# First two channel groups of an input projection computed side by side, with earlier requests for weights and rows

## The chip, the cores and the metric

The kernel runs on one core of a Trainium2 chip. The metric is the device time of one execution in microseconds (us). Five engines take part, each with its own instruction queue that runs in order: PE (TensorE: matmuls and transposes), ACT (ScalarE), DVE (VectorE), POOL (GpSimd) and SP (SyncE, which here only requests DMA transfers). An instruction that has to wait holds up everything behind it in its queue.

## The reference

One layer of a bidirectional encoder on 2048 rows of 1024 channels. Two head groups share one input projection: four mLSTM heads and a Hyena operator (long two-sided convolutions by FFT). An output projection and an MLP follow.

```python
hn = rms_norm(x, norm_mix_pre)
proj = (hn @ w_in).astype(f32)                       # 1024 -> 3600 columns
cv = short_conv3(proj[..., :N_CONV], conv_w, conv_b) # the first 2560 columns, 3 taps along the rows
q, k = silu(cv[..., 0:512]), silu(cv[..., 512:1024]) * D ** -0.5
v, o_gate, gates = proj[..., 2560:3072], sigmoid(proj[..., 3072:3584]), proj[..., 3584:3600] + b_gates
h_m = (mlstm_chunkwise(q, k, v, ...) + flip(mlstm_chunkwise(flip(q), ...))) * o_gate
z = cv[..., 1024:1536]                               # Hyena value, then two gates
z = cv[..., 1536:2048] * two_sided_fft_conv(z, filt[:, 0, 0], filt[:, 1, 0], fb[0])
z = cv[..., 2048:2560] * two_sided_fft_conv(z, filt[:, 0, 1], filt[:, 1, 1], fb[1])
mix = concat([group_rms(h_m), group_rms(z)]) @ w_out
x = x + rms_norm(mix, norm_mix_post)
x = x + rms_norm(square(relu(rms_norm(x) @ w_mlp_in)) @ w_mlp_out)
```

## The kernel before

**Normalisation (`normalise`, L489).** The 2048 rows are 16 tiles of 128 rows. A tile is fetched on SP (`xt`, four buffers), squared and summed on ACT (L516), scaled on DVE (L520), and turned by eight PE transposes (L484) in two halves of four; each half is copied out of PSUM by ACT as a rounded high part (L486) and by DVE as the low part (L487). Four tiles make one row block: `hn[b]`, b = 0 to 3, high and low. The PSUM ring of the transposes holds three halves, so a fourth half waits until ACT and DVE have emptied the first. The short convolution's weights (`cw`, four loads with single elements of 4 bytes) are requested in this stage too.

**Input projection (`convolved`, L559).** 2560 of the columns are 20 channel groups of 128. One block is a group times a row block: 8 steps of k, each three matmuls (L159 low weights, L160 low rows, L161 high times high), so 24 matmuls of 512 columns. Blocks run group by group, and within a group over the four row blocks. ACT starts the convolution of a finished block (L590), DVE adds the two side taps (L596), four PE transposes turn it (L617, the first 12 groups), ACT copies it out (L626), POOL stores it. `in_weights` (L530) fetches a group's weights in two halves (`wf`, two buffers), POOL scales them by the norm's weights (L543), ACT and DVE split them into high and low (L166, L169).

**Fillers and leads.** `project` is a Python generator: the 80 blocks, then `values_project` (the other 1040 columns, 64 blocks of 24 matmuls of 260 columns, in four sets, the first of which needs 4 weight parts to begin), each step yielding a cost. It is the filler beside three leads. During `normalise` every even step p takes three steps of it (one block, L527). Beside `filters` (the Hyena filter spectra; its small matmuls stand at L393) and `long_conv` (the two long convolutions) the function `drive` (L217) advances the filler until its summed cost has caught up with the lead's:

```python
self.drive(work, (1.55 * n for n in self.filters(c2, consts)))
with tc.manual_schedule():
    self.drive(work, self.long_conv(hyp, hy, early))
    for _ in work:
        pass
```

What filler is left when `long_conv` is through is emitted behind it. At the end of `long_conv` its buffers are given back, and `head_loads` requests the k, v and q of mLSTM head 0, 1 MB each, into that space; `turned` then transposes k (L912). The mLSTM stage follows (state updates L932, scores L964, outputs L981 and L982), fed by broadcast loads `mb` and `qs` of 0.5 MB each, whose space is that of the projection's tiles. Before `manual_schedule` a scheduler sets the order of the instructions on each engine; inside it the program's order stands.

Of the kernel before, what the change touches and what calls it, by code (L numbers as in the profile page):

```python
# [8 lines left out]
F32 = mybir.dt.float32  # L9
F32R = mybir.dt.float32r  # L10
AF = mybir.ActivationFunctionType
ALU = mybir.AluOpType
# [135 lines left out]
class Builder:  # L148
# [340 lines left out]
    def normalise(self, c, conv):  # L489

        tc, io = self.tc, self.io
        act, dve = self.act, self.dve
        wk = c.enter_context(tc.tile_pool(name="nwk", bufs=2))
        ps = c.enter_context(tc.tile_pool(name="nps", bufs=3, space=PSUM, side="right"))
        xs = {}

        def fetch(t):
            xs[t] = wk.tile([128, D], F32, tag="xt", name="xt", bufs=4)
            self.load(xs[t], io["x"][0, 128 * t:128 * t + 128, :])

        fetch(0)
        fetch(1)
        self.load(self.nw, io["norm_mix_pre"].rearrange("(k p) -> p k", p=128))
        for p in range(9):
            if p == 2:
                for n in range(3):
                    self.load(self.cw[:, :, n], io["conv_w"][n].rearrange("(t p) -> p t", p=128))
                self.load(self.cw[:, :, 3], io["conv_b"].rearrange("(t p) -> p t", p=128))
            if p < 8:
                if p < 7:  # L510
                    fetch(2 * p + 2)
                    fetch(2 * p + 3)
                ss = wk.tile([128, 2], F32, tag="ss", name="ss")
                for i in range(2):
                    junk = wk.tile([128, D], F32, tag="junk", name="junk", bufs=1)
                    act.activation(junk, xs[2 * p + i], AF.Square, accum_out=ss[:, i:i + 1])  # L516
                r = self.rstd(wk, ss, D, 2, "pre")
                for i in range(2):
                    xt = xs[2 * p + i]
                    dve.tensor_scalar(xt, xt, r[:, i:i + 1], None, ALU.mult)  # L520
            if p > 0:
                for i in range(2):
                    t = 2 * p - 2 + i
                    self.transpose_split(ps, xs.pop(t), *self.hn[t // 4], 128 * (t % 4), "tp", 3)
                if p % 2 == 0:
                    for _ in range(3):
                        next(conv)  # L527
            yield 5.0

# [29 lines left out]
    def convolved(self, cts, then):  # L559

        wk, hn, cw = self.pw, self.hn, self.cw
        pe, dve, act, pool = self.pe, self.dve, self.act, self.pool
        n = 4 * len(cts)
        fetched, weights, pts, ys, sts = {}, {}, {}, {}, {}

        def ahead(c, step):

            if c >= len(cts):
                next(then)
                return  # L570
            fetch, chunk, m = self.in_weights(128 * cts[c], 128)
            if step == 0:
                fetched[c] = [fetch(q) for q in range(m)]
            else:
                weights.setdefault(c, []).append(chunk(fetched[c][step - 1]))

        def of(i):
            return cts[i // 4], i % 4

        def block(i, ks):  # L580
            ct, b = of(i)
            if ks[0] == 0:
                pts[i] = self.pp.tile([128, 512], F32, tag="pp", name="pt")
            for k in ks:
                self.mm3(pts[i], self.row_block(weights[i // 4], k), (hn[b][0][:, k, :], hn[b][1][:, k, :]), k == 0, k == 7)

        def centre(i):
            ct, b = of(i)
            yc = ys[i] = wk.tile([128, 512], F32, tag="yc", name="yc", bufs=4)
            act.activation(yc, pts[i], AF.Identity, scale=cw[:, ct, 1:2], bias=cw[:, ct, 3:4])  # L590

        def sides(i):
            (ct, b), pt, yc = of(i), pts[i], ys[i]

            def add(y, at, p, src, w):
                dve.scalar_tensor_tensor(y[:, at], p[:, src], cw[:, ct, w:w + 1], y[:, at], ALU.mult, ALU.add)  # L596

            if b > 0:

                add(ys[i - 1], slice(511, 512), pt, slice(0, 1), 2)  # L600
                add(yc, slice(0, 1), pts.pop(i - 1), slice(511, 512), 0)
            add(yc, slice(1, 512), pt, slice(0, 511), 0)
            add(yc, slice(0, 511), pt, slice(1, 512), 2)
            if b == 3:
                pts.pop(i)

        def gated(i):
            if of(i)[0] < 8:
                act.activation(ys[i], ys[i], AF.Silu)

        def turn(i):
            ct, b = of(i)
            if ct < 8:
                return
            pt = sts[i] = self.pp.tile([128, 4, 128], F32, tag="ptt", name="ptt", bufs=1)
            for q in range(4):
                pe.transpose(pt[:, q, :], ys[i][:, 128 * q:128 * q + 128], self.eye)  # L617

        def stored(i):
            (ct, b), yc = of(i), ys.pop(i)  # L620
            if ct < 8:
                self.load(self.qk[ct // 4][ct % 4][:, 512 * b:512 * b + 512], yc)
                return
            which, cc = (ct - 8) // 4, 128 * (ct % 4)
            st = wk.tile([128, 520], F32, tag="vst", name="vst")[:, 0:512].rearrange("p (q c) -> p q c", q=4)
            act.copy(st, sts.pop(i))  # L626

            dst = self.vp[which].rearrange("h (b a) c -> (h b) a c", a=32)
            for e in range(2):
                pool.dma_start(dst[:, 8 * b + e:8 * b + 8:2, cc:cc + 128], st[64 * e:64 * e + 64])  # L630

        for step in range(3):
            ahead(0, step)
        for i in range(n + 3):
            live, b = i < n, i % 4
            if live:
                block(i, range(0, 3))
            if 1 <= i <= n:
                centre(i - 1)
            if i >= 3:  # L640
                turn(i - 3)
            if live and b == 1:
                ahead(i // 4 + 1, 0)
            yield 2.04 if live else next(then)
            if live:
                block(i, range(3, 6))
            if 1 <= i <= n:
                sides(i - 1)
            if i >= 3:
                stored(i - 3)  # L650
            if live and b > 1:
                ahead(i // 4 + 1, b - 1)
            yield 2.04 if live else next(then)
            if live:
                block(i, range(6, 8))
            if 2 <= i <= n + 1:
                gated(i - 2)
            yield 1.36 if i < n - 1 else 1.36 * live + next(then)

    def values_project(self):  # L660
# [1157 lines left out]
```

## Time and profile before

| | us |
|---|---|
| median of 3 runs (2784.33 to 2790.24) | 2786.06 |
| profiled execution | 2789.98 |
| its span | 2787.9 |
| PE busy | 2617.9 (94%) |
| DVE, ACT, POOL busy | 1530.7, 1223.3, 1199.6 |
| granted TensorE clock, mean | 0.973 |

The span is what the trace covers; the profiled execution was 2.1 us longer than it. PE is busy in 94% of the span, so what can be won or lost is mainly the time in which PE waits or runs at the lower clock (a granted clock of 1.00 is 2.4 GHz; the other level is 1.2 GHz). The stages follow one another: normalisation until about 70 us, projection beside filters until about 386, projection beside the long convolutions until about 1075, mLSTM until about 1240, output projection, and the MLP from about 1510 on.

### The profile page before, as it was taken

What the parts mean: (1) busy time and instruction counts of PE and PEld (TensorE: products, weight loads), DVE (VectorE), ACT (ScalarE), POOL (GpSimd) and SP (SyncE); (2) the same over time, 40 slices, a digit from 0 to 9 for tenths busy, and PEclk for the clock granted to TensorE, in tenths of its full rate; (3) what the DMA queues carried; (4) which work ended last, traced back from release to release, by engine and by line L of the source; (5) the groups of instructions that cost most, each with busy time, mean ns of one, the idle gap of its engine ahead of it and who ended that gap; (6) DMA issues with size and microseconds to landing.
All of it is one profiled execution on the core that took longest, in us unless ns stands there. A gap on an engine that the chain in (4) does not pass through costs nothing. (4 is left out here: it accounts for less than half of the span.)

```text
span 2787.9 us, 35849 instructions
## 1 busy us (share of the span) xinstructions
PE 2617.9 (94%) x12422; PEld 2140.6 (77%) x12422; DVE 1530.7 (55%) x2593; ACT 1223.3 (44%) x2237; POOL 1199.6 (43%) x946
## 2 busy tenths in 40 slices
PE   6999999999899998888996999989999999999998
PEld 5778877777677888776775788868888888888876
DVE  5676643777436664664443454564445443443478
ACT  6355543655434444543332445455445233232244
POOL 1221124554215542424565877777774251310232
PEclk8999999999999999999998999989999999999999
DMA  6233346565556656955665444464445653444546
GB/s 168 61 99 106 106 138 201 183 194 169 189 192 176 186 164 227 267 187 187 212 214 198 143 159 143 156 223 141 157 159 201 222 181 114 113 144 153 194 152 226
DMA packets 307189, 474.24 MB, mean 170 GB/s; under 512 B 37814, under 2 KB 166198, under 8 KB 305984
## 3 DMA queue, kind: packets, MB, share of 16 engines
q1 hardware_dynamic: 231952, 333.24, 38.4%
q10 hardware_dynamic: 70304, 125.98, 12.1%
q0 software_dynamic: 4752, 12.72, 2.1%
q8 instruction: 99, 1.62, 0.2%
q14 instruction: 82, 0.67, 0.1%
HBM read 297.65 MB, written 174.20 MB: 169 GB/s over the span
## 5 line engine op out<-in xcount | busy, mean ns | idle before, releaser
L166 ACT CAST cb<-m 128x1024 fp32r<-128x1024 f32 (+1 forms) x346 | 281.8, 850 | 446.4 <-PE pm L159 385.7
L169 DVE TENSOR_TENSOR cb<-m,cb 128x1024 fp32r<-128x1024 f32 (+1 forms) x222 | 238.9, 1113 | 300.4 <-ACT cb L166 290.6
L159 PE MATMUL pm<-hm,cb 128*128 128x512 f32 x896 | 354.4, 396 | 15.0 <-issue 8.3
L160 PE MATMUL pm<-hm,cb 128*128 128x512 f32 x896 | 353.8, 395 | 13.3 <-POOL hm L169 9.6
L161 PE MATMUL pm<-hm,cb 128*128 128x512 f32 x896 | 352.4, 393 | 0.0
L160 PE MATMUL pm<-cb 128*128 128x512 f32 x880 | 343.9, 391 | 6.4 <-DVE cb L169 6.4
L159 PE MATMUL pm<-cb 128*128 128x512 f32 x880 | 342.7, 390 | 1.0 <-DVE cb L169 1.0
L161 PE MATMUL pm<-cb 128*128 128x512 f32 x880 | 343.1, 390 | 0.0
L169 POOL TENSOR_TENSOR cb<-m,cb 128x1024 fp32r<-128x1024 f32 x124 | 270.4, 2193 | 53.4 <-ACT cb L166 53.4
L1539 DVE TENSOR_TENSOR m<-pm,m 128x512 f32<-128x512 f32 x224 | 154.0, 690 | 243.3 <-PE pm L161 232.5
L159 PE MATMUL pt<-hn,w 128*128 128x512 f32 x640 | 270.9, 423 | 1.0 <-ACT hn L486 0.9
L169 POOL TENSOR_TENSOR raw<-raw,hi 128x512 fp32r<-128x512 f32 x160 | 205.4, 1296 | 129.5 <-ACT hi L166 118.3
L160 PE MATMUL pt<-hn,w 128*128 128x512 f32 x640 | 254.9, 398 | 0.3 <-DVE hn L487 0.2
L161 PE MATMUL pt<-hn,w 128*128 128x512 f32 x640 | 253.6, 396 | 0.0
L159 PEld LDWEIGHTS pm<-hm,cb 128*128 128x128 f32 x896 | 171.0, 191 | 53.2 <-issue 10.0
L160 PEld LDWEIGHTS pm<-hm,cb 128*128 128x128 f32 x896 | 171.0, 191 | 51.4 <-POOL hm L169 11.3
L160 PEld LDWEIGHTS pm<-cb 128*128 128x128 f32 x880 | 165.6, 188 | 43.8 <-DVE cb L169 9.4
L161 PEld LDWEIGHTS pm<-hm,cb 128*128 128x128 f32 x896 | 171.0, 191 | 35.5
L159 PEld LDWEIGHTS pm<-cb 128*128 128x128 f32 x880 | 165.4, 188 | 35.9 <-ACT junk L1728 1.4
L161 PEld LDWEIGHTS pm<-cb 128*128 128x128 f32 x880 | 165.6, 188 | 34.1
L1543 ACT ACTIVATE m<-m 128x512 f32<-128x512 f32 x128 | 80.5, 630 | 219.6 <-DVE m L1539 211.7
L630 POOL DMA_DIRECT2D vp<-vst x96 | 61.2, 642 | 236.4 <-ACT vst L626 235.1
(323 smaller groups left out, 5699.0 us busy)
## 6 DMA issues: line engine op xcount, KB each, us to landing
ga<-m ACTq DMA_DIRECT2D x96, 512.0 KB, 3.8
m<-ga SPq DMA_DIRECT2D x96, 512.0 KB, 3.7
d<-st ACTq DMA_DIRECT2D x64, 512.0 KB, 3.3
m<-in_w_mlp_in_dram SPq DMA_DIRECT2D x62, 512.0 KB, 4.6
m<-in_w_mlp_out_dram SPq DMA_DIRECT2D x114, 256.0 KB, 4.0
raw<-d SPq DMA_DIRECT2D x96, 256.0 KB, 2.8
xt<-in_x_dram SPq DMA_DIRECT2D x32, 512.0 KB, 5.6
dk<-kst SPq DMA_DIRECT2D x32, 512.0 KB, 3.3
```

Source lines behind the costliest of these rows:

```text
L159: pe.matmul(ps, w[1], x[0], start=first, stop=False)
L160: pe.matmul(ps, w[0], x[1], start=False, stop=False)
L161: pe.matmul(ps, w[0], x[0], start=False, stop=last)
L166: self.act.copy(hi, src)
L169: (eng_lo or self.dve).tensor_tensor(lo, src, hi.bitcast(F32), ALU.subtract)
L630: pool.dma_start(dst[:, 8 * b + e:8 * b + 8:2, cc:cc + 128], st[64 * e:64 * e + 64])
L1539: dve.tensor_tensor(dst, a, b, ALU.add)
L1543: act.activation(g, g, AF.Relu)
```

## The change

`convolved` runs over an explicit sequence: the first two groups go side by side, block (0, b) followed by block (1, b) for each row block b, and the other 18 groups as before. Turning and storing a block now follow a list of finished blocks. The weights of both groups are requested and prepared in a first step of the generator, which `normalise` takes before its loop, behind the fetches of the first four tiles; and each even p takes six steps (two blocks) instead of three. The total of matmuls is the same.

```diff
--- before.py
+++ after.py
@@ -501,13 +501,16 @@
         fetch(0)
         fetch(1)
         self.load(self.nw, io["norm_mix_pre"].rearrange("(k p) -> p k", p=128))
+        fetch(2)
+        fetch(3)
+        next(conv)
         for p in range(9):
...
             if p < 8:
-                if p < 7:
+                if 0 < p < 7:
                     fetch(2 * p + 2)
                     fetch(2 * p + 3)
...
                 if p % 2 == 0:
-                    for _ in range(3):
+                    for _ in range(6):
                         next(conv)
             yield 5.0
...
-        n = 4 * len(cts)
+
+        seq = [(c, b) for b in range(4) for c in range(2)] + [(c, b) for c in range(2, len(cts)) for b in range(4)]
+        n = len(seq)
...
-        def block(i, ks):
-            ct, b = of(i)
+        def block(at, ks):
+            c, b = at
             if ks[0] == 0:
-                pts[i] = self.pp.tile([128, 512], F32, tag="pp", name="pt")
+                pts[at] = self.pp.tile([128, 512], F32, tag="pp", name="pt")
             for k in ks:
-                self.mm3(pts[i], self.row_block(weights[i // 4], k), (hn[b][0][:, k, :], hn[b][1][:, k, :]), k == 0, k == 7)
...
+                self.mm3(pts[at], self.row_block(weights[c], k), (hn[b][0][:, k, :], hn[b][1][:, k, :]), k == 0, k == 7)
...
             if b > 0:
 
-                add(ys[i - 1], slice(511, 512), pt, slice(0, 1), 2)
-                add(yc, slice(0, 1), pts.pop(i - 1), slice(511, 512), 0)
+                add(ys[c, b - 1], slice(511, 512), pt, slice(0, 1), 2)
+                add(yc, slice(0, 1), pts.pop((c, b - 1)), slice(511, 512), 0)
+                done.append((c, b - 1))
...
-        for step in range(3):
-            ahead(0, step)
-        for i in range(n + 3):
-            live, b = i < n, i % 4
+        for c in range(2):
+            for step in range(3):
+                ahead(c, step)
+        yield 0.0
+        done, leaving = [], None
+        for i in range(n + 4):
+            live = i < n
+            c, b = seq[i] if live else (0, 0)
             if live:
-                block(i, range(0, 3))
+                block(seq[i], range(0, 3))
             if 1 <= i <= n:
-                centre(i - 1)
-            if i >= 3:
-                turn(i - 3)
-            if live and b == 1:
-                ahead(i // 4 + 1, 0)
+                centre(seq[i - 1])
+            if done:
+                leaving = done.pop(0)
+                turn(leaving)
+            if live and b == 1 and c > 0:
+                ahead(c + 1, 0)
             yield 2.04 if live else next(then)
             if live:
-                block(i, range(3, 6))
-            if 1 <= i <= n:
-                sides(i - 1)
-            if i >= 3:
-                stored(i - 3)
-            if live and b > 1:
-                ahead(i // 4 + 1, b - 1)
+                block(seq[i], range(3, 6))
+            new = sides(seq[i - 1]) if 1 <= i <= n else []
+            if live and b > 1 and c > 1:
+                ahead(c + 1, b - 1)
+            if live and b == 3 and c == 1:
+                ahead(2, 1)
             yield 2.04 if live else next(then)
             if live:
-                block(i, range(6, 8))
-            if 2 <= i <= n + 1:
-                gated(i - 2)
+                block(seq[i], range(6, 8))
+            if live and b == 3 and c == 1:
+                ahead(2, 2)
+            for at in new:
+                gated(at)
+            done += new
+            if leaving:
+                stored(leaving)
+                leaving = None
             yield 1.36 if i < n - 1 else 1.36 * live + next(then)
```

Where the rows stand now, on two engines and at three places. First SP at the start of the program (`xt` are the rows, `wf` raw weights, `cw` the convolution's weights, `w_304`, `w_305`, `w_347`, `w_348` filter weights). Before:

```order
L231 DMA xt<-in_x_dram 128x1024 x2
L231 DMA nw<-in_norm_mix_pre_dram 128x8x1
L231 DMA xt<-in_x_dram 128x1024 x2
L231 DMA cw<-in_conv_w_dram 128x20x1 x3
L231 DMA cw<-in_conv_b_dram 128x20x1
L231 DMA wf<-in_w_in_dram 128x4x128 x2
L231 DMA xt<-in_x_dram 128x1024 x2
L231 DMA w_304<-in_filt_w_dram 33x64
```

and with the change:

```order
L231 DMA xt<-in_x_dram 128x1024 x2
L231 DMA nw<-in_norm_mix_pre_dram 128x8x1
L231 DMA xt<-in_x_dram 128x1024 x2
L231 DMA wf<-in_w_in_dram 128x4x128 x2
L231 DMA cw<-in_conv_w_dram 128x20x1 x3
L231 DMA cw<-in_conv_b_dram 128x20x1
L231 DMA xt<-in_x_dram 128x1024
L231 DMA wf<-in_w_in_dram 128x4x128 x2
L231 DMA xt<-in_x_dram 128x1024
L231 DMA w_347<-in_filt_w_dram 33x64
```

Group 0's weights have moved ahead of `cw`; the fifth row tile, group 1's weights and the sixth tile stand behind it.

Second, PE at the first blocks (`hn_89` and `hn_90` are the high and low part of row block 0, `hn_91` the high part of row block 1). Before, with one group's weights `w_224` and `w_225`:

```order
L484 MATMUL ptp<-eye,xt 128x128 x32
L159 MATMUL pt<-hn_89,w_225 128x512
L160 MATMUL pt<-hn_90,w_224 128x512
L161 MATMUL pt<-hn_89,w_224 128x512
...
L484 MATMUL ptp<-eye,xt 128x128 x32
L159 MATMUL pt<-hn_91,w_225 128x512
```

and with the change, where `w_123` and `w_124` belong to group 0, `w_137` and `w_138` to group 1:

```order
L484 MATMUL ptp<-eye,xt 128x128 x32
L159 MATMUL pt<-hn_89,w_124 128x512
L159 MATMUL pt<-hn_89,w_138 128x512
L160 MATMUL pt<-hn_90,w_123 128x512
L161 MATMUL pt<-hn_89,w_123 128x512
...
L160 MATMUL pt<-hn_90,w_137 128x512
...
L484 MATMUL ptp<-eye,xt 128x128 x12
L622 MATMUL ptt<-eye,yc 128x128 x3
L484 MATMUL ptp<-eye,xt 128x128 x20
L159 MATMUL pt<-hn_91,w_124 128x512
```

Two blocks (48 matmuls) now stand between two sets of 32 transposes, and the second matmul of all already reads group 1's weights.

Third, PE at the end of the long convolutions (`pu` and `pi` are the last data spectrum and its way back, `pt<-w..,hn..` the filler, `ptk` the turned k, `pS` and `pv` mLSTM). Before, the way back stands ahead of 168 filler matmuls:

```order
L1133 MATMUL pi<-z,ci 128x512
L841 MATMUL pg<-eye,qt 128x128
L159 MATMUL pt<-w_9617,hn_94 128x260
...
L912 MATMUL ptk<-eye,k 128x128 x4
L159 MATMUL pt<-w_9673,hn_96 128x260
...
L912 MATMUL ptk<-eye,k 128x128 x4
L964 MATMUL pS<-q,k 128x128 x7
```

and with the change behind the last of them:

```order
L161 MATMUL pu<-hi,c 128x512
L159 MATMUL pt<-w_9464,hn_96 128x260
...
L161 MATMUL pt<-w_9469,hn_95 128x260
L1148 MATMUL pi<-z,ci 128x512 x2
L927 MATMUL ptk<-eye,k 128x128 x8
L947 MATMUL pv<-v,kw_10346 128x129 x4
L927 MATMUL ptk<-eye,k 128x128 x4
```

No filler stands between `pi` and the turned k any more.

## Rows read from the trace of the kernel before

**Rows 1.** Windows: stretch, length, busy (count) per engine, clock, DMA share, GB/s.

```profile
11.20:75.00 63.80, 50.18 (x236) 39.24 (x237) 40.88 (x71) 40.46 (x76) 9.08 (x10) 0.87 0.57 155
101.30:380.00 278.70, 278.58 (x1252) 223.52 (x1251) 187.33 (x401) 144.01 (x242) 54.08 (x76) 1.00 0.33 98
1075.00:1105.00 30.00, 20.32 (x140) 18.98 (x138) 15.29 (x50) 16.14 (x51) 13.11 (x20) 0.89 0.72 230
1105.00:1205.00 100.00, 83.16 (x666) 80.42 (x665) 67.41 (x290) 52.49 (x177) 44.32 (x51) 0.93 0.90 273
```

**Rows 2.** Timeline, SP's queue at the start: start, duration, engine, line, operation.

```profile
4.12 7.58 SPq L231 DMA_DIRECT2D cw<-in_conv_w_dram  x3
13.60 2.75 SPq L231 DMA_DIRECT2D wf<-in_w_in_dram  x2
16.48 0.89 SPq L231 DMA_DIRECT2D xt<-in_x_dram  x2
```

**Rows 3.** DMA view, first 40 us: GB/s in each microsecond.

```profile
GB/s 0 39 149 274 352 353 147 393 418 178 5 5 5 8 3 7 31 303 198 265 369 407 392 160 0 258 283 1 8 17 17 1 0 0 82 299 201 315 213 274
```

**Rows 4.** Timeline, waits ahead of the first block (idle time and releaser in brackets).

```profile
19.64 0.62 ACT L166 CAST w<-wf 128x512 fp32r<-128x512 f32 x1 [4.14 <-POOL wf L543]
22.90 1.11 PE L484 MATMUL ptp<-eye,xt 128*128 128x128 f32 x4 [5.15 <-DVE hn L487]
```

**Rows 5.** Timeline, PE in the first block.

```profile
24.18 0.80 PE L159 MATMUL pt<-hn,w 128*128 128x512 f32 x1 [0.17 <-ACT hn L486]
29.84 0.39 PE L159 MATMUL pt<-hn,w 128*128 128x512 f32 x1
30.07 0.40 PE L160 MATMUL pt<-hn,w 128*128 128x512 f32 x1
```

**Rows 6.** Windows, PE alone: the three stretches of transposes between blocks.

```profile
32.40:39.09 6.69, 4.81 (x34) 1.00 0.56 169
45.27:56.09 10.82, 6.62 (x38) 0.73 0.70 202
62.55:68.61 6.06, 4.71 (x34) 1.00 0.19 43
```

**Rows 7.** Windows of L159 alone, then L393: PE and PEld.

```profile
24.00:101.50 77.50, 28.67 (x63) 12.77 (x64) 0.92 0.41 116
24.00:101.30 77.30, 5.11 (x10) 1.91 (x10) 0.92 0.41 116
```

**Rows 8.** Timeline, PE in the long convolutions.

```profile
748.20 0.79 PE L159 MATMUL py<-hi,c 128*128 128x512 f32 x1 [4.98 <-ACT hi L166]
844.11 0.50 PE L159 MATMUL pk<-hi,c 128*128 128x512 f32 x1 [2.86 <-POOL c L169]
```

**Rows 9.** Timeline, the end of the long convolutions on DVE, ACT and SP.

```profile
1048.44 0.68 DVE L1103 TENSOR_TENSOR z<-pu,z 64x512 f32<-64x512 f32 x1 [1.45 <-PE pu L161]
1051.34 0.69 DVE L1111 TENSOR_TENSOR z<-z,pu 128x512 f32<-128x512 f32 x1
1055.53 0.58 ACT L1139 COPY st<-pi 128x512 f32<-128x512 f32 x1
1056.14 0.33 ACTq L234 DMA_DIRECT2D d<-st  x1
1058.89 0.33 SPq L231 DMA_DIRECT2D k<-qk  x1
```

**Rows 10.** Windows of L160 alone, behind the last `pi`.

```profile
1054.10:1074.90 20.80, 15.83 (x56) 10.56 (x56) 1.00 0.66 219
```

**Rows 11.** DMA view, 1050 to 1090 us: GB/s in each microsecond.

```profile
GB/s 176 266 0 16 0 66 29 401 94 66 106 434 434 286 313 292 346 442 410 319 246 0 124 143 0 0 170 178 182 125 182 222 380 342 211 154 258 283 313 420
```

**Rows 12.** Timeline, PE at the start of the mLSTM stage.

```profile
1077.01 0.68 PE L932 MATMUL pv<-v,kw 128*128 128x129 f32 x4
1092.49 0.44 PE L912 MATMUL ptk<-eye,k 128*128 128x128 f32 x2 [3.00 <-DMA k<-qk]
1101.23 0.51 PE L932 MATMUL pv<-v,kw 128*128 128x129 f32 x2 [4.52 <-DMA v<-vo]
```

More of the change, by code (lines that the diff above doesn't have):

```diff
@@ L575, in ahead, with centre, sides @@
                 weights.setdefault(c, []).append(chunk(fetched[c][step - 1]))
-        def of(i):
-            return cts[i // 4], i % 4
-        def block(i, ks):
-            ct, b = of(i)
+        def block(at, ks):
+            c, b = at
             if ks[0] == 0:
-                pts[i] = self.pp.tile([128, 512], F32, tag="pp", name="pt")
+                pts[at] = self.pp.tile([128, 512], F32, tag="pp", name="pt")
             for k in ks:
-                self.mm3(pts[i], self.row_block(weights[i // 4], k), (hn[b][0][:, k, :], hn[b][1][:, k, :]), k == 0, k == 7)
[L587 to L593, printed above, removed]
+                self.mm3(pts[at], self.row_block(weights[c], k), (hn[b][0][:, k, :], hn[b][1][:, k, :]), k == 0, k == 7)
+        def centre(at):
+            ct = cts[at[0]]
+            yc = ys[at] = wk.tile([128, 512], F32, tag="yc", name="yc", bufs=4)
+            act.activation(yc, pts[at], AF.Identity, scale=cw[:, ct, 1:2], bias=cw[:, ct, 3:4])
+        def sides(at):
+            (c, b), pt, yc, done = at, pts[at], ys[at], []
             def add(y, at, p, src, w):
-                dve.scalar_tensor_tensor(y[:, at], p[:, src], cw[:, ct, w:w + 1], y[:, at], ALU.mult, ALU.add)
+                dve.scalar_tensor_tensor(y[:, at], p[:, src], cw[:, cts[c], w:w + 1], y[:, at], ALU.mult, ALU.add)
             if b > 0:
-                add(ys[i - 1], slice(511, 512), pt, slice(0, 1), 2)
-                add(yc, slice(0, 1), pts.pop(i - 1), slice(511, 512), 0)
+                add(ys[c, b - 1], slice(511, 512), pt, slice(0, 1), 2)
+                add(yc, slice(0, 1), pts.pop((c, b - 1)), slice(511, 512), 0)
+                done.append((c, b - 1))
             add(yc, slice(1, 512), pt, slice(0, 511), 0)
@@ L604, in sides, with gated, turn, stored @@
             if b == 3:
[L605 to L613, printed above, removed]
+                pts.pop(at)
+                done.append(at)
+            return done
+        def gated(at):
+            if cts[at[0]] < 8:
+                act.activation(ys[at], ys[at], AF.Silu)
+        def turn(at):
+            if cts[at[0]] < 8:
                 return
-            pt = sts[i] = self.pp.tile([128, 4, 128], F32, tag="ptt", name="ptt", bufs=1)
+            pt = sts[at] = self.pp.tile([128, 4, 128], F32, tag="ptt", name="ptt", bufs=1)
             for q in range(4):
-                pe.transpose(pt[:, q, :], ys[i][:, 128 * q:128 * q + 128], self.eye)
-        def stored(i):
-            (ct, b), yc = of(i), ys.pop(i)
+                pe.transpose(pt[:, q, :], ys[at][:, 128 * q:128 * q + 128], self.eye)
+        def stored(at):
+            ct, b, yc = cts[at[0]], at[1], ys.pop(at)
             if ct < 8:
@@ L625, in stored @@
             st = wk.tile([128, 520], F32, tag="vst", name="vst")[:, 0:512].rearrange("p (q c) -> p q c", q=4)
-            act.copy(st, sts.pop(i))
+            act.copy(st, sts.pop(at))
             dst = self.vp[which].rearrange("h (b a) c -> (h b) a c", a=32)
```

## The prediction

> **What bounds the kernel now.** I read the page's busy times first: PE is busy in 94% of the span, so only the places count where PE waits or has the lower clock. The windows by stage then show which these are. Between 101.30 and 380 PE is busy for 278.58 of 278.70 us at full clock [rows 1]: a change of order there can win nothing. Three places are left. In the normalisation, 11.20 to 75.00, PE is busy for 50.18 of 63.80 us, and the granted clock is 0.87 [rows 1]. In the long convolutions the waits show a few stalls of 3 to 5 us where the filler changes its weights [rows 8]. And the mLSTM stage is DMA's: in 1105 to 1205 PE is busy for 83.16 of 100 us while the DMA engines are at 0.90 and 273 GB/s [rows 1]. The timeline, the DMA view and the windows of single lines, read in that order, give the prices at the three places.
>
> The change adds no matmul and no bytes. It moves four blocks (96 matmuls, 96 × 0.23 = 22 us by the spacing of [rows 5]) from behind the normalisation into it. So everything that the filler does later stands 22 us earlier against its leads, and the filler runs out earlier.
>
> **The start.** I compare the moment at which 192 projection matmuls (8 blocks) are through. Before, the 64th weight load of L159 falls in the stretch to 101.5; by then 10 halves of filter matmuls, 5.1 us, have run too [rows 7]. Without these the moment is 96.4.
>
> After, step by step. Before, the weights waited on SP behind `cw`: three of its loads held SP for 7.58 us, and the weights went out at 13.60 [rows 2]; in the slices from 10 to 16 the traffic fell to 31 GB/s and less [rows 3], some 7 us in which those loads of single elements moved nearly nothing. Now group 0's weights (0.5 MB) go ahead of `cw`. The first ten slices moved 2.3 MB [rows 3]; half a megabyte more at some 350 to 400 GB/s lands at about 11.4. The 7 us of `cw` then reach to 18.4, and the fifth row tile and group 1's weights stand behind them. ACT's first weight cast waited 4.14 us for POOL until 19.64, and PE waited 5.15 us until 22.90 for DVE to empty a transposed half [rows 4], so ACT's and DVE's work between them, not the weights alone, sets the first block, which began at 24.18 [rows 5]. After, the casts of group 0 come early, but two of group 1 (0.62 us each [rows 4]) may stand ahead of the copies of `hn`: 25.4. That is a loss of 1.2 us; without it a gain of a few is possible.
>
> The first twelve matmuls ran at half rate, 24.18 to 29.84, then one every 0.23 us [rows 5]. Two blocks take 5.7 + 36 × 0.233 = 14.1 us, until 39.5. Then come three stretches of transposes, 6.69, 10.82 and 6.06 us before [rows 6]. In each PE is busy for only 4.7 to 6.6 us, and the second had a clock of 0.73: row tiles came late. Now there are 11.2 us of matmuls between two stretches instead of 5.6, so ACT, DVE and the row tiles have twice the time. For the second I take 8.4, the mean of its own 10.82 and the 6.06 of the third; for the first 6.7; for the third 6.7, as copies of turned blocks (0.6 us of ACT) now come between. With 3 × 48 × 0.233 = 33.6 us of matmuls the eight blocks end at 39.5 + 21.8 + 33.6 = 94.9. **Gain 1.5 us.** If each stretch shrank to its busy time at full clock (4.7 each) it would be 9 us; if the second stayed at 10.82 and row tile and weights behind `cw` cost another 1.4 us (0.5 MB at 360 GB/s), it would be a loss of 2. Range: loss of 2 to gain of 9.
>
> **The long convolutions.** Filler that takes new weights stalls PE where ACT or POOL must split them beside the lead's own chunks: 4.98 us at 748.20 and 2.86 at 844.11 are the largest [rows 8]. Shifted by 22 us of filler, the change to `values_project` falls ahead of the first `py`, where the filler runs alone and long, and the change of its last set away from the first `pk`. I count 3 of these 7.8 us as **gained**. The ends: all of it (8), or a loss of 2 where splitting meets other chunks.
>
> **The end of the long convolutions.** This is the price. Before, 168 filler matmuls stood behind the last `pi` (56 of L160, three of a kind), and covered 20.8 us [rows 10]. Under them ran: the copy of `pi`, its store, 2.75 us until the store had landed, and then the loads of k, v and q at 1058.89 [rows 9]. After, as the order shows, no filler is left there, and PE waits. From the last `pu` on: DVE's product, 1048.44 to 1052.03, 3.6 us; `pi` 0.6; copy 0.6; issue and landing 3.1: k is requested 7.9 us behind `pu`, and 1.4 us of filler is all that PE has. The 3 MB of k, v and q took the slices 1059 to 1070, 3.7 MB with what else ran, 308 GB/s [rows 11]: about 3.5 us for each, 12 in all. So `ptk` can start 11.4 us behind `pu`, `pv` about 15.5 to 16, `pS` with q at 20. Before, `pv` began at 1077.01 [rows 12], 2.1 us behind the end of the filler. The gross loss is 14 (by `pv`) to 18 (by q).
>
> Much of it comes back. Before, the two streams `mb` and `qs` were requested behind the filler, from 1075 on, and DMA moved in the slices 1071 to 1085 only 2.4 MB in 15 us [rows 11]; at 308 GB/s these take 8. After, these small loads go out while PE waits. Then PE's waits for k and v of the next head, 3.00 and 4.52 us [rows 12], have slack for 7.5 us as far as DMA is ahead. The bounds of what comes back are 7.5 (the two waits) and about 13 (the 7 us of slow slices and 6 for 2 MB loaded ahead). Loss: 1 to 11; if next to nothing comes back in a stage at 0.90 DMA share [rows 1], up to 14. I take **6**, the middle of 1 and 11.
>
> The Trainium skill, "DMA: Bandwidth & Descriptors", section "Rules for kernel authors", says to issue a transfer early, compute, and wait late, so that its fixed cost is hidden; the change does the opposite here. By its fit in "Anatomy of one DMA" (2.0 us and bytes at 436 GB/s) the three loads would be there 9.2 us behind the request, an estimate, and the loss 3 us smaller than by the 12 us of the row. The trace's rate was lower, and I go by it.
>
> The clock: after the wait of 5.15 us [rows 4] the twelve matmuls to 29.84 ran at 1.2 GHz and cost 2.9 us more than at 2.4 [rows 5], and in 1075 to 1105, with its waits, the granted clock was 0.89 [rows 1]. A wait of 10 us before `ptk` will bring that back, but what runs slowly there (`ptk`, the first `pv`) waits for v and q anyway; I add nothing, and keep 2.9 us in the range. The Trainium skill, "TensorE: Matmul & The Clock Gate", section "HAM oscillation — how this bites in real kernels", describes this, waits for DMA between matmuls that each end in a cold start; by it the sum would be 2.9 us higher.
>
> **The sum.** −1.5 − 3 + 6 = +1.5 us. On the profiled execution (2789.98, 2.1 us of it outside the span) that is 2791.5; that execution lies 3.9 us above the median of the runs, so on the median it is 2786.06 + 1.5 = 2787.5.
>
> **The rivals.** *A, slower: the uncovered loads.* k, v and q are paid for at the end of the long convolutions, and only PE's two waits for the next head give back: 18 − 7.5 = 10.5, with a gain of 1 at start and middle together about 2796. It decides when q ends the wait rather than k or v. For it: the stage is full of transfers at 0.90 [rows 1], so nothing runs faster later. Against it: the slow slices of [rows 11].
> *B, faster: the normalisation fills up.* The three stretches lose most of what PE waits in them (gain 6), the stalls at 748 and 844 go nearly wholly (gain 5), and the end costs 3, as the stage is held by DMA, whose total is the same: −8, 2778. For it: 23.6 us of stretches with 16 us of work in them [rows 6]. Against it: `cw` still clogs 7 us of queue, now in front of the fifth row tile.
> *C: the request ahead does nothing.* Group 1's weights stand behind `cw`, and PE's second matmul already reads them; if they land at 20 or later, and are split after that, the first block starts at 27 or later and the start gains nothing. With the middle and the end as above it is +3, inside my forecast's range.
>
> **How the numbers follow.** Forecast (2781 to 2794 by itself; C is part of it) 0.44, A 0.30, B 0.26. A change under 0.2%, 5.6 us, can't be told from none here. Faster by more than that: B and a little of the forecast, 0.28; slower: A and a little of the forecast, less the part of A below 5.6, 0.30; within it 0.42. The range of 8 in 10 takes in the middles of A and B and some beyond each: 2777 to 2800.
>
> **What would show it.** In the profile after: eight blocks through at about 95 us, not 101.5 less filter work; the second stretch of transposes at 8 us; no stall near 5 us at the first `py`; a gap of PE of about 10 us between `pi` and `ptk`, released by the load of k, and `pS` some 20 us behind the last `pu`; the waits of 3.00 and 4.52 us smaller. I am wrong if the gap is not there, if the mLSTM stage takes up all of it or none, or if the stretches keep their length with the blocks doubled.

## The result, and the profile after

The changed kernel takes 2797.07 us (median of 6 runs, 2793.64 to 2801.11), the kernel before 2783.42 in the runs beside it; the ratio is 1.0043 with a 95% interval of 1.0031 to 1.0056, that is +12 us (the two medians lie 13.7 us apart). The forecast was 2787.5, range 2777 to 2800, "no change" the likeliest; what came is rival A's time (2796), not the forecast's.

The two profiled executions differ by less than the medians: the one after took 2794.66, the one before 2789.98, which is long for its kernel (beside the 12 experiments that follow, its medians were 2784 to 2786). So differences of stages between the two traces are only good to some 4 us, and lean towards a gain; other traces are set beside them below.

The head of the page after:

```profile
span 2792.3 us, 35829 instructions
PE 2606.7 (93%) x12422; PEld 2132.8 (76%) x12422; DVE 1528.4 (55%) x2593; ACT 1219.1 (44%) x2235; POOL 1203.0 (43%) x946
```

PE does the same work (x12422) and stands idle for 185.6 us of the span instead of 170.0.

**The start** came as forecast. Windows of L159 alone (stretch, length, PE and PEld with counts, clock, DMA share, GB/s), which answer to [rows 7]:

```profile
25.00:94.60 69.60, 26.43 (x64) 12.51 (x64) 0.95 0.40 119
```

All 64 matmuls of L159 lie ahead of 94.6, and the last of the 192 ends at 94.8 (forecast 94.9). The first two matmuls of the timeline, and the windows of PE alone over the three stretches of transposes, which answer to [rows 5, 6]:

```profile
25.91 1.22 PE L159 MATMUL pt<-hn,w 128*128 128x512 f32 x2 [0.71 <-ACT hn L486]
```

```profile
40.31:46.77 6.46, 4.90 (x36) 1.00 0.67 209
58.30:64.96 6.66, 4.86 (x39) 1.00 0.55 173
76.60:82.73 6.13, 5.28 (x45) 1.00 0.21 43
```

The stretches are 6.5, 6.7 and 6.1 us, and the 10.82 at a clock of 0.73 has gone. They are 2.5 us shorter in all than forecast, and the blocks between and behind them 1.6 us longer; the moment at which all is through came out right partly because these two cancel.

**The long convolutions.** PE's waits between 380 and 1000 (engine, line, what it waited for, us in total, times, the longest), before and after:

```profile
PE py L159 <- ACT hi L166: 12.3, 7, 5.0
PE ptt L617 <- ACT vst L626: 1.9, 1, 1.9
PE pt L159 <- ACT w L166: 1.9, 1, 1.9
```

```profile
PE pt L159 <- ACT w L166: 10.2, 4, 2.7
PE py L159 <- ACT hi L166: 8.8, 6, 2.3
PE ptt L622 <- ACT vst L631: 6.1, 1, 6.1
```

The stalls at `py` shrink, as forecast [rows 8]; but the filler itself now waits 10.2 us for its weights, and the turned blocks 6.1 us (ahead of the first `pk`). Windows of PE from the first `pk` (a chunk's filter spectrum in the long convolutions) to the last, before and after:

```profile
491.97:1042.94 550.97, 522.61 (x2706) 0.98 0.59 183
513.11:1059.26 546.15, 518.20 (x2805) 0.98 0.60 185
```

PE stands idle for 28.4 us of the first and 28.0 us of the second: in sum the waits are what they were.

**The end** is where the time goes. The timeline after, which answers to [rows 9, 12]:

```profile
1064.14 0.39 PE L161 MATMUL pu<-hi,c 128*128 128x512 f32 x1
1066.00 0.38 SPq L231 DMA_DIRECT2D mb<-mrow  x1
1066.94 0.46 SPq L231 DMA_DIRECT2D qs<-irow  x1
1070.07 0.33 ACTq L234 DMA_DIRECT2D d<-st  x1
1081.77 0.33 SPq L231 DMA_DIRECT2D k<-qk  x1
1086.80 1.08 PE L927 MATMUL ptk<-eye,k 128*128 128x128 f32 x4 [17.39 <-DMA k<-qk]
1090.81 1.93 PE L947 MATMUL pv<-v,kw 128*128 128x129 f32 x8
1095.45 1.06 PE L979 MATMUL pS<-q,k 128*128 128x128 f32 x8
```

PE waits 17.39 us for k. I had the load requested 7.9 us behind `pu`; it is requested 17.2 us behind its end (1064.53). The reason stands between: `mb` and `qs` went out from 1066.00 on, and the last store (`d<-st`), issued at 1070.07 beside them, let SP go on only at 1081.77. That is 11.7 us; before it was 2.75 [rows 9]. SP's waits between 1060 and 1245 name this store:

```profile
SPq L231 <- DMA d<-st: 12.5, 1, 12.5
```

The DMA view of 40 us from 1060 answers to [rows 11]:

```profile
GB/s 7 16 0 53 401 70 0 176 170 214 196 183 135 88 229 250 258 246 221 264 229 27 66 205 418 386 327 302 290 399 393 410 467 418 346 389 166 141 157 287
```

While the 2 MB of `mb` and `qs` and the store ran (1067 to 1080) the engines moved 88 to 264 GB/s; when k, v and q ran, with the first loads of head 1 beside them (1084 to 1095), 290 to 467. And the windows of PE in the mLSTM stage, which answer to [rows 1]:

```profile
1075.00:1105.00 30.00, 15.95 (x118) 0.68 0.91 283
1105.00:1205.00 100.00, 81.42 (x629) 0.91 0.86 275
```

The clock is 0.68 in the first 30 us. The same 100 us show PE no busier than before (81.42, before 83.16), but the stage stands later in them. So I also take it whole, PE alone from the first `pv` to the first matmul of the output projection, before and after:

```profile
1077.01:1231.72 154.71, 122.74 (x936) 0.92 0.78 238
1090.81:1236.45 145.64, 122.53 (x949) 0.93 0.77 241
```

The stage is 9.1 us shorter, nearly all of it waiting. PE's waits for loads between 1060 and 1245, before and after, show where it comes from:

```profile
PE ptk L912 <- DMA k<-qk: 9.0, 2, 6.0
PE pv L932 <- DMA v<-vo: 5.9, 2, 4.5
```

```profile
PE ptk L927 <- DMA k<-qk: 17.4, 1, 17.4
PE pv L947 <- DMA v<-vo: 4.7, 1, 4.7
PE pS L979 <- DMA q<-qk: 2.5, 1, 2.5
```

Before, these are waits inside the stage: for head 1's k and v (3.00 and 4.52 [rows 12]) and for head 3's (5.96 and 1.34). After, head 1's two are gone and head 3's k too; left are 4.7 us for head 3's v and 2.5 for a q. The 17.4 us stand ahead of the stage.

### The profile page after: what moved, and what is told of

Read it like the earlier page. It is cut to its first block, busy times and chain, and to the rows that moved or that the text cites. A ratio compares the mean times of both kernels' runs of the same rounds, so it can differ in the third digit from the quotient of the medians.

```text
span 2792.3 us, 35829 instructions
## 1 busy us (share of the span) xinstructions
PE 2606.7 (93%) x12422; PEld 2132.8 (76%) x12422; DVE 1528.4 (55%) x2593; ACT 1219.1 (44%) x2235; POOL 1203.0 (43%) x946
## 5 line engine op out<-in xcount | busy, mean ns | idle before, releaser
L159 PE MATMUL pm<-hm,cb 128*128 128x512 f32 x896 | 353.9, 395 | 16.5 <-issue 9.3
L160 PE MATMUL pm<-hm,cb 128*128 128x512 f32 x896 | 353.6, 395 | 13.8 <-POOL hm L169 9.9
L160 PE MATMUL pm<-cb 128*128 128x512 f32 x880 | 343.3, 390 | 6.9 <-DVE cb L169 6.9
L159 PE MATMUL pm<-cb 128*128 128x512 f32 x880 | 342.2, 389 | 1.0 <-DVE cb L169 1.0
L159 PE MATMUL pt<-hn,w 128*128 128x512 f32 x640 | 270.0, 423 | 2.1 <-ACT hn L486 2.1
L160 PE MATMUL pt<-hn,w 128*128 128x512 f32 x640 | 254.5, 398 | 0.5 <-DVE hn L487 0.4
L159 PEld LDWEIGHTS pm<-hm,cb 128*128 128x128 f32 x896 | 170.9, 191 | 54.3 <-issue 11.1
L160 PEld LDWEIGHTS pm<-hm,cb 128*128 128x128 f32 x896 | 170.9, 191 | 51.5 <-POOL hm L169 11.1
L160 PEld LDWEIGHTS pm<-cb 128*128 128x128 f32 x880 | 165.2, 188 | 44.4 <-DVE cb L169 10.3
L159 PEld LDWEIGHTS pm<-cb 128*128 128x128 f32 x880 | 165.1, 188 | 35.8 <-ACT junk L1743 1.4
L599 DVE SCALAR_TENSOR_TENSOR yc<-pt,cw,yc 128x511 f32<-128x511 f32 (+1 forms) x280 | 135.1, 515 | 86.2 <-ACT yc L592 84.2
```

What stands on the lines that cost most here:

```text
L159: pe.matmul(ps, w[1], x[0], start=first, stop=False)
L160: pe.matmul(ps, w[0], x[1], start=False, stop=False)
L599: dve.scalar_tensor_tensor(y[:, at], p[:, src], cw[:, cts[c], w:w + 1], y[:, at], ALU.mult, ALU.add)
```

## The experiments

For each trace I set the same instruction beside that of before, and took off what more filler had run ahead of it (0.233 us for a matmul of 512 columns, 0.119 for 260, from their spacing). What is left is gained (−) or lost. "MLP" is the start of the MLP's matmuls (`pm`, 1506.4 us before), and "end" is that column less the one of the last `pk`. Ratios are of the runs, with 95% intervals.

| kernel | first `pk` | last `pk` | MLP | end | ratio |
|---|---|---|---|---|---|
| changed kernel | −1.2 | −6.5 | +4.0 | 10.5 | 1.0043 [1.0031, 1.0056] |
| e1 paced at 0.945 | +0.7 | +8.9 | +13.1 | 4.2 | 1.0051 [1.0039, 1.0063] |
| e2 before, drained | −0.3 | −9.7 | +0.4 | 10.1 | 1.0010 [1.0000, 1.0020] |
| e3 three steps | −10.8 | −13.5 | −15.1 | −1.6 | 0.9961 [0.9949, 0.9973] |
| e4 no early request | −1.9 | −4.5 | +5.1 | 9.6 | 1.0041 [1.0029, 1.0054] |
| e5 paced in filters | −5.8 | −8.7 | −8.9 | −0.2 | 0.9981 [0.9969, 0.9992] |
| e6 three steps, paced | −10.3 | −11.3 | −10.5 | 0.8 | 0.9988 [0.9978, 0.9998] |
| e7 before, requests | −3.7 | −4.0 | −4.9 | −0.9 | 0.9998 [0.9988, 1.0007] |
| e8 three steps, no early | −12.6 | −15.6 | −17.3 | −1.7 | 0.9963 [0.9952, 0.9975] |
| e9 drained at the end | +1.1 | −2.6 | +9.3 | 11.9 | 1.0050 [1.0037, 1.0064] |
| e10 four steps | −12.7 | −8.1 | −6.1 | 2.0 | 1.0003 [0.9993, 1.0013] |
| e11 five steps | −8.1 | −6.6 | −5.2 | 1.4 | 0.9996 [0.9987, 1.0005] |
| e12 store undisturbed | −1.6 | −3.0 | +3.1 | 6.1 | 1.0045 [1.0032, 1.0058] |

The columns are single executions, the ratio is not. e9 is the kernel before up to the last `pk` but one, and yet its trace gains 3.7 us from the first to the last `pk`; e4 and e12, which have the order of the changed kernel there, gain 2.6 and 1.4. So most of the 5.3 us that the changed kernel seems to gain there is the trace of before.

**e1_paced.** Give back the lost cover by slower filler beside the long convolutions.

```diff
-                self.drive(work, self.long_conv(hyp, hy, early))
+                self.drive(work, (0.945 * n for n in self.long_conv(hyp, hy, early)))
```

> The changed kernel with one edit: beside the long convolutions the filler is paced at 0.945 of the lead's cost instead of 1. By the order, 168 filler matmuls again stand behind the last pi, as before the change. Theory (the loss is the loads of k, v and q that have lost their cover): PE's wait at the first ptk falls from 17.4 us to under 1, pS begins about 2 us behind the filler's end, and the gain of 6.5 us that the changed kernel has at the last pu (1.2 of it at the first pk) remains in part: ratio to before 0.997 to 1.000 (2775 to 2784). Rival (blocks side by side or the earlier requests cost something elsewhere, and the loads only move): the ratio stays at 1.003 to 1.005. Rival (the mLSTM stage is held by DMA whatever stands ahead of it): the wait goes, but the stage ends at the same time, ratio 1.002 or more.

Measured: 1.0051. The 17.4 us wait is gone (8.4 us in two waits, the longest 4.7), the "end" column falls from 10.5 to 4.2, and the kernel is no faster. My first theory fails in its plain form: what was restored at the end was missed on the way. PE's waits between 380 and 1060:

```profile
PE py L159 <- ACT hi L166: 15.2, 9, 4.2
PE pt L159 <- ACT w L166: 11.2, 3, 6.8
```

So I changed the theory: the filler is one stock of cover. The change spends four blocks (22 us) of it during the normalisation, and where e1 saves them, beside the long convolutions, something else lies bare.

**e2_before_drained.** The same line in the kernel before, with 1.053.

> The kernel before with one edit: beside the long convolutions the filler is paced at 1.053 of the lead's cost, so that by the order 24 filler matmuls stand behind the last pu and none behind the last pi; normalisation and projection are as before. Theory of the uncovered loads: a wait of 15 to 18 us at the first ptk as in the changed kernel, about half of it made up in the mLSTM stage, ratio 1.003 to 1.007. Rival (the loss is the change's own, in the projection): no loss, ratio 0.999 to 1.001.

Measured: 1.0010. The wait at `ptk` is there (15.6 us), and the end costs 10.1 us, as in the changed kernel, but the denser filler wins 9.7 us on the way (last `pk`; PE stands idle 22.8 us between first and last `pk`, before 28.4): the end's price exists without the change, and cover moved to the middle pays most of it back. The theory had the wait right and the ratio wrong; the ratio is the rival's, and its reason, that there is no loss at the end, is not.

**e3_three_steps.** The changed kernel with three steps per even p.

```diff
-                    for _ in range(6):
+                    for _ in range(3):
```

> The changed kernel with one edit: during the normalisation each even p takes three steps of the filler (one block) instead of six. The groups still go side by side and the first requests still go ahead, but the filler is no longer four blocks ahead; by the order 168 filler matmuls stand behind the last pi. Theory: the end of the long convolutions is as before, the wait at ptk is gone; the start loses the 1.2 us gained or keeps them: ratio 0.998 to 1.001. Rival (side by side costs elsewhere): ratio 1.003 or more.

Measured: 0.9961, 11 us faster than before, 23 faster than the change. The end is covered, and the start wins 10.8 us, which I had not expected. Windows of PE alone, from the first block to the end of the transposes: before, changed, e3.

```profile
24.18:68.61 44.43, 36.73 (x176) 0.86 0.54 162
```

```profile
25.91:82.73 56.82, 52.50 (x260) 0.94 0.40 123
```

```profile
25.34:61.40 36.06, 35.09 (x181) 0.93 0.54 171
```

PE waits 7.7, 4.3 and 1.0 us. Before and e3 have about the same matmuls in their windows (x176 and x181), and e3's is 8.4 us shorter. With three steps the scheduler lays matmuls of group 1's block, which needs no later rows, between the transposes. PE of e3 in the timeline:

```profile
33.91 1.47 PE L484 MATMUL ptp<-eye,xt 128*128 128x128 f32 x12
35.13 0.48 PE L160 MATMUL pt<-hn,w 128*128 128x512 f32 x1
35.45 0.39 PE L161 MATMUL pt<-hn,w 128*128 128x512 f32 x1
36.37 1.21 PE L484 MATMUL ptp<-eye,xt 128*128 128x128 f32 x8
37.33 0.48 PE L159 MATMUL pt<-hn,w 128*128 128x512 f32 x1
```

With six, both blocks are through before the next transposes, and the stretches stay closed.

**e4_no_early_request.** The changed kernel with the fetches in their old order and `next(conv)` behind the loads of `cw`.

> The changed kernel without the earlier requests: row tiles fetched in the order of before and the weights of both groups requested behind cw; blocks side by side and six steps as in the change. Theory: the first block begins 1 to 4 us later than in the changed kernel (25.9 us), the rest is the same, the wait at ptk stays: ratio to before 1.004 to 1.007. Rival (the earlier requests themselves delay the row tiles and cost time): ratio under 1.003.

Measured: 1.0041, the same as the change within its interval. The first matmul starts at 23.75, not later but earlier, so the theory's "1 to 4 us later" is wrong, though its ratio is met. No effect of the requests shows.

**e5_paced_in_filters.** The changed kernel, the four blocks saved where PE was full, beside the filter spectra.

```diff
-                self.drive(work, (1.55 * n for n in self.filters(c2, consts)))
+                self.drive(work, (1.38 * n for n in self.filters(c2, consts)))
```

> The changed kernel with one edit: beside the filter spectra the filler is paced at 1.38 of the lead's cost instead of 1.55; by the order the same amount of filler (1446 matmuls) is then spent before the first pk as in the kernel before, and 168 matmuls stand behind the last pi. Revised theory (filler is a fixed stock of cover, and the four blocks spent early are missed later; beside the filter spectra PE was busy for 278.6 of 278.7 us, so there they can be saved at no price): PE stays busy in that stretch, the gain of 3 us at the first filter matmul remains to the end, ratio to before 0.998 to 1.000. Rival (each stretch needs the cover it had; slower filler there opens stalls as it did beside the long convolutions): ratio 1.003 or more. Rival (side by side itself costs later): ratio 1.003 with no new stall beside the spectra.

Measured: 0.9981; against the changed kernel's 1.0043 that is 17 us for one number. PE, 101 to 380 us:

```profile
101.30:380.00 278.70, 278.70 (x1249) 1.00 0.32 97
```

There was no stall to open there, and the end is covered (−0.2). This bears out the revised theory: it is not the blocks side by side that cost, but that the filler ran ahead of its leads.

**e6_three_steps_paced.** e3 with 1.45 beside the spectra and 1.03 beside the long convolutions.

> The version with three steps per even p, with the filler paced at 1.45 instead of 1.55 beside the filter spectra and at 1.03 instead of 1 beside the long convolutions (180 matmuls behind the last pi). Theory: filler saved where PE is full serves the stretch of the second long convolution, where 1.053 won 5 to 9 us in the kernel before; the end keeps its cover: ratio 0.993 to 0.996. Rival (no spare beside the spectra): ratio 0.996 or more, with waits there.

Measured: 0.9988, slower than e3, the rival's ratio, but without the rival's waits: beside the spectra nothing is lost (−10.3 at the first `pk`). The middle gains nothing either, unlike e2. So the pace is not a simple dial. It may be that it changes which filler instruction meets which chunk of the lead; that is not shown, and I did not settle why e2 won there and e6 did not.

**e7_before_requests.** The kernel before, with the first four tiles and group 0's weights requested ahead of the loop (`fetch(2)`, `fetch(3)`, `next(conv)`).

> The kernel before with the earlier requests alone: the first four row tiles and group 0's weights are requested ahead of the normalisation's loop; groups one after the other, one block per even p. Theory (the 10.5 us won with three steps come from group 1's block, which the scheduler can put between the transposes, since it needs no later rows): little is won here, 0 to 3 us, ratio 0.999 to 1.000, and the three stretches of transposes stay closed. Rival (the requests win it): ratio 0.996 to 0.997.

Measured: 0.9998. No gain shows from the requests alone.

**e8_three_steps_no_early.** e4 with three steps.

> The version with three steps per even p and groups side by side, with the requests in the order of before (row tiles, cw, then the weights of both groups). Theory (side by side wins it): nearly all stays, ratio 0.996 to 0.998. Rival (the requests win it): ratio 0.999 to 1.001.

Measured: 0.9963, as e3. With e4 and e7 this says that what is won comes from side by side with three steps. e3 and e8 beat both kernels. (That blocks are turned and stored from a list belongs to every version with the groups side by side; no run has it alone.)

**e9_drained_at_the_end.** The kernel before, with the filler drained at one place near the end.

```diff
-                yield 1.3
+                yield 1.3 + (22.0 if o == 1 and j == 30 else 0.0)
```

> The kernel before with one edit: at one place near the end of the second long convolution (the step for j = 30) 22 more units of filler are called for, so that by the order 12 filler matmuls stand behind the last pu and none behind the last pi, as in the changed kernel; everything up to there is as before. It measures the price of the uncovered loads alone. Revised theory (of a gross loss of 20 us behind the last pu only some 5 come back in the mLSTM stage): wait at the first ptk 15 to 18 us, ratio 1.004 to 1.006. Rival (more than half comes back, as my sum had it, and the changed kernel loses elsewhere): ratio 1.001 to 1.003.

Measured: 1.0050, 14 us (10 to 18 by the interval): the price of the uncovered end alone. Its timeline shows the same picture as the changed kernel's:

```profile
1074.03 0.33 ACTq L234 DMA_DIRECT2D d<-st  x1
1085.78 0.33 SPq L231 DMA_DIRECT2D k<-qk  x1
1090.92 1.09 PE L912 MATMUL ptk<-eye,k 128*128 128x128 f32 x4 [17.54 <-DMA k<-qk]
```

Again the store takes 11.7 us, and PE waits 17.5.

**e10_four_steps** and **e11_five_steps**: the same line as e3, with 4 and 5.

> The changed kernel with four steps per even p instead of six (three: ratio 0.9961, six: 1.0043). By the order 108 filler matmuls, about 13 us, stand behind the last pi. Theory (the loss is filler missing at the end; the loads need some 15 us of cover): a wait of a few us at ptk, start nearly as with three steps, ratio 0.996 to 0.999. Rival (the loss comes with any block that is run ahead in the normalisation): halfway to six steps or more, ratio 1.000 or more.

> The changed kernel with five steps per even p instead of six. By the order 48 filler matmuls, about 6 us, stand behind the last pi. Theory: 9 to 11 us wait at ptk, part of the start's gain gone, ratio 1.000 to 1.003. Rival (the start alone decides, with stretches of transposes closed by whole blocks): as six steps, 1.004.

Measured: 1.0003 and 0.9996. Four steps came out slower than the theory said, at its rival's ratio; five steps lie just under the theory's range, within their interval, and by that rival they should have been slower than four. Their traces keep most of e3's start (−12.7 and −8.1 at the first `pk`) and pay little at the end (2.0 and 1.4), but four steps lose 4.6 us between first and last `pk`, where e3 gains 2.7. So the price at the end alone does not explain them, and the middle counts too. What makes four steps slower than five is not settled: the profiled execution of four (2780.74) was the fastest of its 11, 6.8 us below their median, so its trace does not show what the others lost.

**e12_store_undisturbed.** The changed kernel, with `mb`, `qs` and head 1's loads held behind k and q by a copied column.

```diff
+        hold = lambda t: h == 1 and self.pool.tensor_copy(t, self.mh[0]["q"][:, 0:1])
...
+        if h == 0 and g < 2:
+            pool.tensor_copy(mb[:, 0, 0, 0:1], m["k"][:, 0:1])
+            pool.tensor_copy(qs[:, 0, 0:1], m["k"][:, 0:1])
```

> The changed kernel with the first broadcast loads of the mLSTM stage (two of mb, two of qs, 2 MB) and those of head 1 held back until k and q of head 0 have landed (a copy of one column by POOL makes them wait), so that SP has the order of the kernel before: k, v, q, then mb and qs. Six steps, no filler left, as in the changed kernel. In the changed kernel those loads stood ahead, and the last store (d), on which k waits, took 11.7 us to land instead of 2.75. Theory (half of the price at the end is that delayed store): the store lands in under 4 us, the wait at the first ptk falls from 17.4 us to 8 to 10, and the ratio to 1.000 to 1.003. Rival (the stage is held by the bytes to be moved, in whatever order): the wait shrinks, but the stage ends at the same time, ratio 1.003 to 1.006.

Its timeline:

```profile
1073.57 0.33 ACTq L234 DMA_DIRECT2D d<-st  x1
1076.31 0.33 SPq L231 DMA_DIRECT2D k<-qk  x1
1081.52 1.09 PE L931 MATMUL ptk<-eye,k 128*128 128x128 f32 x4 [8.61 <-issue]
```

The store lands in 2.74 us and PE's wait is halved, 8.6 us, as the theory said (the trace names no releaser for it). The ratio is 1.0045, as the rival said: against the changed kernel's 1.0043 no gain shows. The stage from the first `pv` to the output projection, in e12:

```profile
1085.58:1236.96 151.38, 124.91 (x950) 0.90 0.80 245
```

That is 5.7 us longer than in the changed kernel (145.64): most of what the early store wins is missing behind it, where `mb` and `qs` are now requested (from 1081.50 on). In this trace 4.4 us are left over (column "end", 6.1 against 10.5); the runs don't show them, but their intervals, some 3.6 us to either side, can't rule out a gain of that size. The store's delay is real, but it is not what the bulk of the 12 us hangs on.

## Why the prediction was wrong where it was

**Start, −1.5: right in its sum.** 94.8 against 94.9 for the eight blocks, with the two terms that cancel; −1.2 at the first `pk`, no more than traces with the same order up to there differ by (e2 −0.3, e9 +1.1). Rival C was half true: no effect of the requests shows (e4), but for another reason than theirs, since the first block waits for `hn` and not for weights (`[0.71 <-ACT hn L486]` above).

**Long convolutions, −3: not borne out.** The stalls named did shrink, by 3.5 us at `py`, but the filler's own waits for its weights grew by 8.3 and those of turned blocks by 4.2, and PE's idle time between first and last `pk` is the same (28.4 and 28.0). The trace seems to gain 5.3; the trace of e9 gains 3.7 with nothing changed up to the last `pk` but one. About nothing is left.

**End, +6: the step that failed.** The gross loss of 14 was too small; measured it is 20 (by `pv`: 13.8 later, from 6.5 earlier at the last `pk`). Its mis-sized term is "issue and landing 3.1": the store took 11.7 us, because the loads of `mb` and `qs`, which I had counted only as a gain, went out first. So k was requested 17.2 us behind `pu` and not 7.9, and `pS` stands 31 us behind it and not 20. In e12, with the store undisturbed, k is requested 8.3 us behind `pu`, and the gross loss is 11.6.

"Much of it comes back" was right in size and largely in its way: the stage is 9.1 us shorter than before in the changed kernel and 8.4 in e9 (146.3 us), where I took 8 of 14, and the two waits that I had named, 3.00 and 4.52 us, are gone. What I had not seen is that the two halves of the sum hang together: sending `mb` and `qs` early costs 8.7 of gross loss (20.3 against 11.6 in e12) and gives 5.7 back in the stage, so it is no gain.

What is left of the loss is 10.5 us in the trace, and 14 by the runs of e9 (10 to 18), against the 6 I took. My bound "up to 14 if next to nothing comes back" has the number of e9's runs, but not its reason. By sums: −1.2, about 0, and 14 give +12.8; measured +12.

That the time still lies inside the stated range is owed to the range's width, which took in A. Rival A had the place and the time (2796), in part by luck: its gross loss of 18 and its 7.5 coming back were both some 2 us too small. Its condition, that q ends the wait, did not hold, since k ended it; and its sentence "nothing runs faster later" is not what the windows show.

**What the prediction lacked** is the view of the filler as one stock. It asked at each place what moves by 22 us, and not where those 22 us of cover were idle. They were idle beside the filter spectra [rows 1], where I wrote that an order can win nothing; e5 saves them exactly there and has the 17 us back. And for the start I compared closed stretches of transposes, and did not see that one block less would let the scheduler open them (e3).

## What to carry to other kernels

Work that fills waits is a stock: before spending it earlier, find the stretch in which the engine is full anyway (here 278.6 of 278.7 us) and save it there, and see what it last covered at the end. Where the saved work then helps has to be tried (e5 and e6). Two independent pieces of work side by side pay when the scheduler can lay one into the other's gaps; more of it at once closes the gaps again (at the first `pk` three steps have gained 10.8 us, six 1.2). A wait that is shortened in front of a stage with many transfers need not be a gain (e12: 8.8 us less wait, the ratio the same): look at the stage's end, not at the wait.

## What the runs showed that was not expected

- A store of 512 KB that landed in 2.75 us took 11.7 with 2 MB of broadcast loads issued up to 4 us ahead of it on another queue, in two kernels (the changed one and e9); 2.74 with these held back (e12). For the load that waited on this store, what else was in flight counted more than its own size.
- While those loads and the store ran, the DMA engines moved 88 to 264 GB/s, against 290 to 467 for k, v and q with head 1's first loads.
- PE waited 17.4 us, and the clock of 1075 to 1105 fell to 0.68 (0.89 before [rows 1]). What the lower clock cost by itself no run separates.
- PE's waits for head 1's k and v, 7.5 us before [rows 12], were gone when head 0's loads came late.
